# Splitting the last columns over two paths, and pieces of eight columns in place of four

## The chip, the cores and the metric

One core of one Trainium2 chip. The metric is the device time of one execution in microseconds (us), median over several executions, always compared with executions of the kernel before on the same chip in the same rounds. The profile is one execution taken by the hardware profiler; its span is about 1.7 us shorter than the measured time.

## The reference

The loss of a masked autoencoder: normalise every target patch, take the mean squared difference to the prediction, one number per image.

```python
batch, num_masked, dim = 32, 147, 768            # float32 inputs pred and target
mean = target.mean(axis=-1, keepdims=True)
var = target.var(axis=-1, keepdims=True)
target = (target - mean) / np.sqrt(var + 1e-6)
loss = np.mean((pred - target) ** 2, axis=-1)
return loss.mean(axis=-1).astype(np.float32)     # (32,)
```

## The kernel before

The 4704 patches lie as 36 full "columns" of 128 patches (one per partition) and a rest of 96. A column is 128 x 768 elements. All data is read once: the first target piece as float32 on a plain queue, nearly everything else on GpSimd's queue, which casts to bfloat16 on the way.

Work on a column c goes through four engines. VectorE takes the statistics of the target (two `bn_stats`, one `bn_aggr`), ScalarE the root, VectorE the reciprocal, GpSimd normalises:

```python
def normalise(u, c):                             # on GpSimd
    ...
    pin(nc.gpsimd.tensor_scalar(out=s[:n, so:so + D], in0=til[:n, o:o + D], scalar1=nm, scalar2=r,
                                op0=ALU.add, op1=ALU.mult))
```

Then the difference to the prediction and its square, on one of three paths, named in the list of units: "ACT" (TensorE forms p - s in PSUM with two identity matrices, ScalarE squares), "DVE+ACT" (VectorE subtracts, ScalarE squares), "DVE" (VectorE does both):

```python
def difference(u, d0, w):                        # two SBUF inputs
    ...
    pin(nc.vector.tensor_tensor(out=z[:, :w], in0=til[:, o:o + w], in1=s[:, so + d0:so + d0 + w],
                                op=ALU.subtract))

def square_dve(u, d0, w, dest):                  # reads z twice
    z = zs[u, d0][:, :w]
    pin(nc.vector.scalar_tensor_tensor(out=z, in0=z, scalar=1.0, in1=z, op0=ALU.mult, op1=ALU.mult,
                                       accum_out=dest))
```

The squares' row sums meet in a last small matmul per unit (`acc`), and 32 numbers are copied and written out. The order on each engine is fixed when the kernel is built: a list scheduler gives every operation an estimated duration, data arrival and rank, and emits them in the order of its estimated starts.

Of the kernel before, what the change touches and what calls it, by code (L numbers as in the profile page):

```python
# [7 lines left out]
F32 = mybir.dt.float32  # L8
BF16 = mybir.dt.bfloat16
ALU = mybir.AluOpType  # L10
ACTF = mybir.ActivationFunctionType
# [3 lines left out]
def kernel(  # L15
# [7 lines left out]
    nc = tc.nc  # L23
    pin = tc.keep_in_program_order
    B, N, D = pred.shape
    eps = 1e-6
    P = 128
    J = P // B
    KJ = (N + J - 1) // J
    KM = N - (J - 1) * KJ  # L30
    assert KJ == KM + 1
    RP = B * (J - 1)
    half = D // 2
    BANK = 512
    REST = KM
# [4 lines left out]
    def rows_of(c):  # L40
        return RP if c == REST else P

    data = ctx.enter_context(tc.tile_pool(name="data", bufs=1))
    work = ctx.enter_context(tc.tile_pool(name="work", bufs=16))
    diffs = ctx.enter_context(tc.tile_pool(name="diffs", bufs=4))
    small = ctx.enter_context(tc.tile_pool(name="small", bufs=8))
    singles = ctx.enter_context(tc.tile_pool(name="singles", bufs=1))
    psum = ctx.enter_context(tc.tile_pool(name="psum", bufs=2, space=bass.MemoryType.PSUM))
    psum1 = ctx.enter_context(tc.tile_pool(name="psum1", bufs=1, space=bass.MemoryType.PSUM))


# [3 lines left out]
    def piece(kind, c0, c1, d0=0, d1=D, q="sw"):  # L55
        stream.append((kind, c0, c1, d0, d1, q))

    piece("t", 0, 4, q="hw")
    piece("t", REST, REST + 1, q="hw2")
    piece("t", 4, 8)  # L60
    piece("p", REST, REST + 1)
    piece("t", 8, 12)
    piece("p", 0, 4)
    piece("t", 12, 16)
    piece("t", 16, 20)
    piece("p", 4, 8)
    piece("t", 20, 24)
    piece("t", 24, 28)
    piece("p", 8, 12)
    piece("t", 28, 32)  # L70
    piece("p", 12, 16)
    piece("t", 32, 36)
    for c in range(16, 32, 2):
        piece("p", c, c + 2)
    for c in range(32, 35):
# [6 lines left out]
    groups += [(c, c + 1) for c in range(16, KM, 2)]  # L82


    units = [((c, c + 1), 0, D, "ACT" if c < 18 else "DVE+ACT") for c in range(0, 24, 2)]
    units.insert(2, ((REST,), 0, D, "ACT"))
    units += [((24,), 0, D, "DVE"), ((25,), 0, D, "DVE+ACT"), ((26, 27), 0, D, "DVE+ACT")]
    units += [((c,), 0, D, "ACT" if c % 2 else "DVE") for c in range(28, KM - 1)]
    units += [((KM - 1,), 0, half, "ACT"), ((KM - 1,), half, D, "ACT")]



# [3 lines left out]
    def op(name, engine, dur, needs, fn, rank=0.0, early=0.0):  # L96
        by_name[name] = len(ops)
        ops.append((name, engine, dur, needs, fn, rank, early))
# [13 lines left out]
            KIND[kind].setdefault(c, []).append((d0, d1, til, (c - c0) * w))  # L112


    land, lanes, clock = {}, {"hw": [], "hw2": [], "sw": []}, 2.9
    for i, (kind, c0, c1, d0, d1, q) in enumerate(stream):
        w = (c1 - c0) * (d1 - d0)
        clock += w * rows_of(c0) / P * 0.915 / D + (0.0 if w >= 4 * D else 0.04)
        lanes[q].append(clock + 1.1)
        for c in range(c0, c1):  # L120
            land[kind, c, d0] = clock + 1.1
        k = len(lanes[q])
        op(("load", i), {"hw": "SP", "hw2": "ACT", "sw": "POOL"}[q], 0.6, [], lambda a=stream[i]: load(*a), rank=-1.0,
           early=0.0 if k <= 8 else lanes[q][k - 9] + 0.3)

    def landed(kind, c):
        return max(t for (k, cc, d), t in land.items() if k == kind and cc == c)

    ident = singles.tile([P, P], BF16)
# [25 lines left out]
    def bn(out, parts):  # L155

        n = parts[0].shape[0]
        st = small.tile([P, len(parts), 6], F32, name="st")
        for j, x in enumerate(parts):
            pin(nc.vector.bn_stats(out=st[:n, j, :], in_=x))  # L160
        pin(nc.vector.bn_aggr(out=out, in_=st[:n, :len(parts)]))  # L161

    def stats(g, i):
        n, K = rows_of(g[0]), len(g)
        if i == 0:
            mvs[g] = small.tile([P, K, 2], F32, name="mv")
        if not norm_pix_loss:
            return
        (_, _, til, o), = tbuf[g[i]]
        bn(mvs[g][:n, i], [til[:n, o + a:o + a + half] for a in (0, half)])  # L170
# [20 lines left out]

    for k, g in enumerate(groups):
        for i, c in enumerate(g):
            op(("bn", c), "DVE", 1.26, [], lambda g=g, i=i: stats(g, i), rank=k - 50.0, early=landed("t", c))
        op(("root", k), "ACT", 0.55, [("bn", c) for c in g], lambda g=g: root(g), rank=-1.0)
        op(("recip", k), "DVE", 0.2, [("root", k)], lambda g=g: recip(g), rank=-60.0)

# [16 lines left out]
    zs = {}  # L214
# [4 lines left out]

    def product(u, d0, w, src, so, eye, first):  # L220
        n, z = rows_of(u[0]), zs[u, d0]
        for a in range(0, w, BANK):
            b = min(w, a + BANK)
            pin(nc.tensor.matmul(z[:n, a:b], eye[:n, :n], src[:n, so + a:so + b], start=first, stop=not first))  # L224

    def sub_target(u, d0, w):
        if (u, d0) == units[-1][:2]:
            zs[u, d0] = psum1.tile([P, BANK], F32, name="z_last")
        else:
            zs[u, d0] = psum.tile([P, 3 * BANK], F32, name="z")  # L230
        s, so = sbuf[u[0]]
        product(u, d0, w, s, so + d0, nident, True)

# [7 lines left out]
    def difference(u, d0, w):  # L241

        z = zs[u, d0] = diffs.tile([P, 2 * D], BF16, name="zd")
        s, so = sbuf[u[0]]
        til, o = pred_of(u[0], d0)
        pin(nc.vector.tensor_tensor(out=z[:, :w], in0=til[:, o:o + w], in1=s[:, so + d0:so + d0 + w],  # L246
                                    op=ALU.subtract))

    def square_dve(u, d0, w, dest):
        z = zs[u, d0][:, :w]  # L250
        pin(nc.vector.scalar_tensor_tensor(out=z, in0=z, scalar=1.0, in1=z, op0=ALU.mult, op1=ALU.mult,  # L251
                                           accum_out=dest))

    tail = 5
    n_early = len(units) - 1 - tail
    rl = singles.tile([P, n_early], F32)
    rl_sum = singles.tile([P, 1], F32)
    finals = []
    early_ops, users, seen = [], [], set()
    for k, (u, d0, d1, eng) in enumerate(units):  # L260
        w = len(u) * D if len(u) > 1 else d1 - d0
        arrive = max(t for (kk, c, d), t in land.items() if kk == "p" and c in u and d < d1)
        norms = [("norm", c) for c in u]
        for c in u:
            if c not in seen:
                op(("norm", c), "POOL", 1.02, [("recip", group_of[c])], lambda u=u, c=c: normalise(u, c), rank=k)
                seen.add(c)
        if k < len(units) - tail:
            if u[0] == REST:
                dest = singles.tile([P, 1], F32, name="rl_rest")  # L270
                finals.append((("sq", k), dest, mask_rest, RP))
            else:
                dest = rl[:, len(early_ops):len(early_ops) + 1]
                early_ops.append(("sq", k))
        else:
            dest = singles.tile([P, 1], F32, name=f"rl{k}")
            finals.append((("sq", k), dest, mask, P))
        if eng in ("DVE", "DVE+ACT"):
            op(("diff", k), "DVE", 0.57 * w / D + 0.05, norms, lambda u=u, d0=d0, w=w: difference(u, d0, w), rank=-2.0,
               early=arrive)  # L280
            if eng == "DVE":
                op(("sq", k), "DVE", 1.0 * w / D, [("diff", k)],
                   lambda u=u, d0=d0, w=w, dest=dest: square_dve(u, d0, w, dest), rank=-1.0)
            else:
                op(("sq", k), "ACT", 0.75 * w / D + 0.25, [("diff", k)],
                   lambda u=u, d0=d0, w=w, dest=dest: square_act(u, d0, w, dest), rank=k)
            continue
        op(("subt", k), "PE", 0.37 * w / D, norms + (users[-2:-1] if k < len(units) - 1 else []) + ["ident"],
           lambda u=u, d0=d0, w=w: sub_target(u, d0, w), rank=k + 0.0)
        op(("pred", k), "PE", 0.37 * w / D, [("subt", k)], lambda u=u, d0=d0, w=w: add_pred(u, d0, w), rank=k,  # L290
           early=arrive)
        op(("sq", k), "ACT", 0.73 * w / D + 0.23, [("pred", k)],
           lambda u=u, d0=d0, w=w, dest=dest: square_act(u, d0, w, dest), rank=k)
        users.append(("sq", k))

    acc = psum1.tile([1, B], F32)
    def early_sum():
        junk = singles.tile([P, n_early], F32, name="junk")
        pin(nc.scalar.activation(out=junk, in_=rl, func=ACTF.Copy, accum_out=rl_sum))

    op("rl_sum", "ACT", 0.4, early_ops, early_sum, rank=50.0)
    finals.insert(0, ("rl_sum", rl_sum, mask, P))
    turn = []

    def final(vec, m, n):
        turn.append(n)
        pin(nc.tensor.matmul(acc, vec[:n], m[:n], start=len(turn) == 1, stop=len(turn) == len(finals)))  # L307

    for i, (need, vec, m, n) in enumerate(finals):
        op(("final", i), "PE", 0.2, [need, "masks"], lambda v=vec, m=m, n=n: final(v, m, n), rank=90.0)  # L310


    HOP = 0.15
# [3 lines left out]
    while left:  # L317
        best = None
        for i in left:
            name, engine, dur, needs, fn, rank, early = ops[i]  # L320
            if any(x not in end for x in needs):
                continue
            t = max([free[engine], early] + [end[x] + (0.0 if ops[by_name[x]][1] == engine else HOP) for x in needs])
# [4 lines left out]
        _, i, t = best  # L328
        name, engine, dur, needs, fn, rank, early = ops[i]
# [43 lines left out]
```

## Time and profile before

| | before |
|---|---|
| measured time, 6 runs of the comparison | 77.09 us (77.06 to 77.22) |
| span of the profiled execution | 75.4 us |
| DMA engines | full from 2 us to 71 us |
| VectorE / GpSimd busy | 75% / 72% of the span |
| TensorE / ScalarE busy | 40% / 42% |
| last data packet | 71.20 us |
| start of the final copy | 73.26 us |

The first lines to read are the slices of the DMA engines: a stream that never pauses sets the start of the end, and only what remains after its last packet can be shortened. The prediction below shows them, the end of the chain of waits, and VectorE beside GpSimd (start us, duration us, engine, line, operation). A line of the timeline gives start us, duration us, engine, line, operation.

```profile
63.04 0.55 DVE L246 TENSOR_TENSOR zd<-p,s 128x768 bf16<-128x768 bf16 x1
...
63.27 1.95 POOL L210 TENSOR_SCALAR s<-t,nm,r 128x768 bf16<-128x768 bf16 x1
63.51 0.95 DVE L251 SCALAR_TENSOR_TENSOR zd<-zd 128x768 bf16<-128x768 bf16 x1
```

The POOL line is one normalisation (x1), and it takes 1.95 us instead of 0.98. It began while a difference was running (to 63.59) and 0.24 us before VectorE's square, yet ended 0.97 us late. The difference overlaps it for only about 0.3 us; the rest of the delay lies beside the square, which itself shows nothing.

### The profile page before, as it was taken

What the parts mean: (1) busy time and instruction counts of PE and PEld (TensorE: products, weight loads), DVE (VectorE), ACT (ScalarE), POOL (GpSimd) and SP (SyncE); (2) the same over time, 40 slices, a digit from 0 to 9 for tenths busy, and PEclk for the clock granted to TensorE, in tenths of its full rate; (3) what the DMA queues carried; (4) which work ended last, traced back from release to release, by engine and by line L of the source; (5) the groups of instructions that cost most, each with busy time, mean ns of one, the idle gap of its engine ahead of it and who ended that gap; (6) DMA issues with size and microseconds to landing.
All of it is one profiled execution on the core that took longest, in us unless ns stands there. A gap on an engine that the chain in (4) does not pass through costs nothing.

```text
span 75.4 us, 570 instructions
## 1 busy us (share of the span) xinstructions
PE 30.3 (40%) x87; PEld 8.7 (11%) x88; DVE 56.3 (75%) x148; ACT 32.0 (42%) x73; POOL 54.4 (72%) x77
## 2 busy tenths in 40 slices
PE   0000000038596540688700778287544000348860
PEld 0000000001232110211100211031111000112220
DVE  0000099999999999976999928960999989989940
ACT  1400000210229802289210297239366099799550
POOL 4998205099999999499989898999878799800000
PEclk9999999999999997555555557965995555555555
DMA  0899999999999999999999999999999999999700
GB/s 0 215 424 339 262 192 236 218 209 215 212 215 215 212 216 225 212 209 215 215 212 215 219 212 225 209 212 202 214 215 209 215 210 210 214 205 205 117 0 0
DMA packets 3973, 15.41 MB, mean 204 GB/s; under 512 B 450, under 2 KB 1186, under 8 KB 3842
## 3 DMA queue, kind: packets, MB, share of 16 engines
q0 software_dynamic: 3712, 13.52, 89.2%
q1 hardware_dynamic: 146, 1.57, 5.7%
q10 hardware_dynamic: 112, 0.29, 1.0%
q14 instruction: 3, 0.02, 0.1%
HBM read 28.90 MB, written 0.00 MB: 383 GB/s over the span
## 4 chain that ended last, share of the span: by engine, by line
DMA 60%; DVE 18%; POOL 9%; issue 6%; PE 2%; ACT 1%; POOLq 0%; ACTq 0%
DMA t<-in_target_dram 49%; DVE st L160 14%; DMA p<-in_pred_dram 11%; POOL s L210 8%; DVE mv L161 3%; DVE zd L246 1%; PE acc L307 1%; POOL t L110 1%; PE z L224 1%; ACT z_last L239 1%; PE z_last L224 1%; POOLq L368 0%; DVE r L190 0%; POOL p L110 0%; DVE ob L336 0%
## 5 line engine op out<-in xcount | busy, mean ns | idle before, releaser
L160 DVE BATCH_NORM_STATS2 st<-t 128x6 f32<-128x384 bf16 (+2 forms) x74 | 36.3, 532 | 11.6 <-DMA t<-in_target_dram 11.6
L210 POOL TENSOR_SCALAR s<-t,nm,r 128x768 bf16<-128x768 bf16 (+2 forms) x37 | 38.2, 1040 | 3.2 <-ACT nm L185 2.0
L224 PE MATMUL z<-s,nident 128*128 128x512 bf16 (+4 forms) x36 | 14.6, 511 | 23.3 <-POOL s L210 17.6
L239 ACT ACTIVATE z<-z 128x1536 f32<-128x1536 f32 (+3 forms) x14 | 16.6, 1184 | 6.9 <-PE z L224 6.8
L224 PE MATMUL z<-p,ident 128*128 128x512 bf16 (+4 forms) x35 | 14.2, 542 | 12.1 <-DMA p<-in_pred_dram 12.0
L184 ACT ACTIVATE r<-mv,eps_t 128x2 f32<-128x2 f32 (+2 forms) x15 | 4.4, 293 | 29.5 <-DVE mv L161 28.8
L110 POOL DMA_DIRECT2D p<-in_pred_dram x18 | 10.2, 565 | 2.7 <-DVE st L160 1.0
L246 DVE TENSOR_TENSOR zd<-p,s 128x768 bf16<-128x768 bf16 (+1 forms) x10 | 9.7, 991 | 0.5 <-ACT zd L239 0.3
L161 DVE BATCH_NORM_AGGREGATE mv<-st 128x2 f32<-128x12 f32 (+1 forms) x37 | 7.7, 209 | 1.3
L110 POOL DMA_DIRECT2D t<-in_target_dram x8 | 4.9, 628 | 4.7 <-DMA t<-in_target_dram 3.9
L239 ACT ACTIVATE zd<-zd 128x1536 bf16<-128x1536 bf16 (+1 forms) x5 | 6.7, 1345 | 2.7 <-DVE zd L246 2.7
L224 PEld LDWEIGHTS <-ident 128*128 128x128 bf16 (+1 forms) x37 | 4.7, 126 | 27.2 <-issue 26.2
L224 PEld LDWEIGHTS <-nident 128*128 128x128 bf16 (+1 forms) x37 | 3.4, 114 | 34.6 <-issue 14.4
L251 DVE SCALAR_TENSOR_TENSOR zd<-zd 128x768 bf16<-128x768 bf16 x5 | 4.8, 955 | 0.1
L224 PE MATMUL z_last<-s,nident 128*128 128x384 bf16 x1 | 0.5, 479 | 7.1 <-POOL s L210 7.1
L190 DVE RECIPROCAL r<-r 128x2 f32<-128x2 f32 (+2 forms) x15 | 1.9, 123 | 1.7 <-ACT r L184 1.7
L185 ACT ACTIVATE nm<-mv 128x2 f32<-128x2 f32 (+2 forms) x15 | 2.8, 188 | 0.0
L239 ACT ACTIVATION_READ_ACCUMULATOR z<-z 128x1 f32 (+1 forms) x14 | 2.7, 190 | 0.0
L184 ACT ACT_TABLE_LOAD x1 | 1.3, 1283 | 1.5 <-PEq L354 1.5
L307 PE MATMUL acc<-mask,rl 128*1 128x32 f32 x10 | 1.0, 224 | 0.4 <-ACT z_last L239 0.4
L239 ACT ACTIVATION_READ_ACCUMULATOR zd<-zd 128x1 f32 x5 | 0.9, 187 | 0.0
L336 DVE COPY ob<-acc 1x32 f32<-1x32 f32 x1 | 0.2, 178 | 1.0 <-PE acc L307 1.0
(26 smaller groups left out, 5.8 us busy)
## 6 DMA issues: line engine op xcount, KB each, us to landing
t<-in_target_dram POOLq DMA_DIRECT2D x8, 768.0 KB, 24.5
p<-in_pred_dram POOLq DMA_DIRECT2D x4, 768.0 KB, 27.4
p<-in_pred_dram POOLq DMA_DIRECT2D x8, 384.0 KB, 20.9
t<-in_target_dram SPq DMA_DIRECT2D x1, 1536.0 KB, 8.4
p<-in_pred_dram POOLq DMA_DIRECT2D x3, 192.0 KB, 12.7
t<-in_target_dram ACTq DMA_DIRECT2D x1, 288.0 KB, 9.6
p<-in_pred_dram POOLq DMA_DIRECT2D x2, 96.0 KB, 7.3
p<-in_pred_dram POOLq DMA_DIRECT2D x1, 144.0 KB, 10.4
```

The lines of the kernel that those rows point to most:

```text
L110: pin(eng.dma_start(out=til[:n], in_=src))
L160: pin(nc.vector.bn_stats(out=st[:n, j, :], in_=x))
L161: pin(nc.vector.bn_aggr(out=out, in_=st[:n, :len(parts)]))
L184: pin(nc.scalar.activation(out=r[:n], in_=mv[:n, :, 1], func=ACTF.Sqrt, bias=eps_t[:n], scale=1.0))
L185: pin(nc.scalar.activation(out=nm[:n], in_=mv[:n, :, 0], func=ACTF.Copy, scale=-1.0))
L190: pin(nc.vector.reciprocal(out=rs[g][:n], in_=rs[g][:n]))
L210: pin(nc.gpsimd.tensor_scalar(out=s[:n, so:so + D], in0=til[:n, o:o + D], scalar1=nm, scalar2=r, op0=ALU.add, op1=ALU.mult))
L224: pin(nc.tensor.matmul(z[:n, a:b], eye[:n, :n], src[:n, so + a:so + b], start=first, stop=not first))
L239: pin(nc.scalar.activation(out=z[:n, :w], in_=z[:n, :w], func=ACTF.Square, accum_out=dest[:n]))
L246: pin(nc.vector.tensor_tensor(out=z[:, :w], in0=til[:, o:o + w], in1=s[:, so + d0:so + d0 + w], op=ALU.subtract))
L251: pin(nc.vector.scalar_tensor_tensor(out=z, in0=z, scalar=1.0, in1=z, op0=ALU.mult, op1=ALU.mult, accum_out=dest))
L307: pin(nc.tensor.matmul(acc, vec[:n], m[:n], start=len(turn) == 1, stop=len(turn) == len(finals)))
```

## The change

Its intent: fewer and larger transfers in the first half of the stream, and a shorter end, by cutting the last columns between ScalarE's path (the first 512 elements) and VectorE's (the other 256), in pairs with a strided access where there are two columns. It also lets the statistics of columns 32 to 35 wait behind differences, moves the early sum and the differences of columns 16 and 17 to VectorE, adds a fifth buffer for differences, divides PSUM anew for the split pieces, and re-estimates durations. Its core:

```diff
-    piece("t", 4, 8)
+    piece("t", 4, 12)
     piece("p", REST, REST + 1)
-    piece("t", 8, 12)
-    piece("p", 0, 4)
-    piece("t", 12, 16)
-    piece("t", 16, 20)
-    piece("p", 4, 8)
-    piece("t", 20, 24)
-    piece("t", 24, 28)
+    piece("t", 12, 20)
+    piece("p", 0, 8)
+    piece("t", 20, 28)
+    piece("t", 28, 32)
     piece("p", 8, 12)
 ...
-    units += [((24,), 0, D, "DVE"), ((25,), 0, D, "DVE+ACT"), ((26, 27), 0, D, "DVE+ACT")]
-    units += [((c,), 0, D, "ACT" if c % 2 else "DVE") for c in range(28, KM - 1)]
-    units += [((KM - 1,), 0, half, "ACT"), ((KM - 1,), half, D, "ACT")]
+    units += [((24,), 0, D, "DVE"), ((25,), 0, D, "DVE+ACT")]
+    for u in [(c, c + 1) for c in range(26, KM - 4, 2)] + [(c,) for c in range(KM - 4, KM - 1)]:
+        units += [(u, 0, BANK, "ACT"), (u, BANK, D, "DVE")]
+    units += [((KM - 1,), 0, half, "ACT"), ((KM - 1,), half, D, "DVE")]
 ...
-            op(("bn", c), "DVE", 1.26, [], ..., rank=k - 50.0, early=landed("t", c))
+            op(("bn", c), "DVE", 1.26, [], ..., rank=k - 50.0 if c < 32 else -1.5, early=landed("t", c))
 ...
+            y = til[:, o - d0:o - d0 + K * D].rearrange("p (k d) -> p k d", d=D)[:, :, d0:d0 + e]
+            v = s[:, so:so + K * D].rearrange("p (k d) -> p k d", d=D)[:, :, d0:d0 + e]
 ...
-    op("rl_sum", "ACT", 0.4, early_ops, early_sum, rank=50.0)
+    op("rl_sum", "DVE", 0.2, early_ops, ...tensor_reduce..., rank=-3.0)
```

More of the change, by code (lines that the diff above doesn't have):

```diff
@@ L44 @@
     work = ctx.enter_context(tc.tile_pool(name="work", bufs=16))
-    diffs = ctx.enter_context(tc.tile_pool(name="diffs", bufs=4))
+    diffs = ctx.enter_context(tc.tile_pool(name="diffs", bufs=5))
     small = ctx.enter_context(tc.tile_pool(name="small", bufs=8))
     singles = ctx.enter_context(tc.tile_pool(name="singles", bufs=1))
-    psum = ctx.enter_context(tc.tile_pool(name="psum", bufs=2, space=bass.MemoryType.PSUM))
     psum1 = ctx.enter_context(tc.tile_pool(name="psum1", bufs=1, space=bass.MemoryType.PSUM))
@@ L59 @@
     piece("t", REST, REST + 1, q="hw2")
-    piece("t", 4, 8)
+    piece("t", 4, 12)
     piece("p", REST, REST + 1)
-    piece("t", 8, 12)
-    piece("p", 0, 4)
-    piece("t", 12, 16)
-    piece("t", 16, 20)
-    piece("p", 4, 8)
-    piece("t", 20, 24)
-    piece("t", 24, 28)
+    piece("t", 12, 20)
+    piece("p", 0, 8)
+    piece("t", 20, 28)
+    piece("t", 28, 32)
     piece("p", 8, 12)
-    piece("t", 28, 32)
+    piece("t", 32, 36)
     piece("p", 12, 16)
-    piece("t", 32, 36)
     for c in range(16, 32, 2):
@@ L82 @@
     groups += [(c, c + 1) for c in range(16, KM, 2)]
-    units = [((c, c + 1), 0, D, "ACT" if c < 18 else "DVE+ACT") for c in range(0, 24, 2)]
+    units = [((c, c + 1), 0, D, "ACT" if c < 16 else "DVE+ACT") for c in range(0, 24, 2)]
     units.insert(2, ((REST,), 0, D, "ACT"))
-    units += [((24,), 0, D, "DVE"), ((25,), 0, D, "DVE+ACT"), ((26, 27), 0, D, "DVE+ACT")]
-    units += [((c,), 0, D, "ACT" if c % 2 else "DVE") for c in range(28, KM - 1)]
-    units += [((KM - 1,), 0, half, "ACT"), ((KM - 1,), half, D, "ACT")]
+    units += [((24,), 0, D, "DVE"), ((25,), 0, D, "DVE+ACT")]
+    for u in [(c, c + 1) for c in range(26, KM - 4, 2)] + [(c,) for c in range(KM - 4, KM - 1)]:
+        units += [(u, 0, BANK, "ACT"), (u, BANK, D, "DVE")]
+    units += [((KM - 1,), 0, half, "ACT"), ((KM - 1,), half, D, "DVE")]
     ops, by_name = [], {}
@@ L112, in load @@
             KIND[kind].setdefault(c, []).append((d0, d1, til, (c - c0) * w))
-    land, lanes, clock = {}, {"hw": [], "hw2": [], "sw": []}, 2.9
+    land, lanes, clock = {}, {"hw": [], "hw2": [], "sw": []}, 2.8
     for i, (kind, c0, c1, d0, d1, q) in enumerate(stream):
@@ L193 @@
         for i, c in enumerate(g):
-            op(("bn", c), "DVE", 1.26, [], lambda g=g, i=i: stats(g, i), rank=k - 50.0, early=landed("t", c))
+            op(("bn", c), "DVE", 1.26, [], lambda g=g, i=i: stats(g, i), rank=k - 50.0 if c < 32 else -1.5, early=landed("t", c))
         op(("root", k), "ACT", 0.55, [("bn", c) for c in g], lambda g=g: root(g), rank=-1.0)
@@ L221, in product @@
         n, z = rows_of(u[0]), zs[u, d0]
-        for a in range(0, w, BANK):
-            b = min(w, a + BANK)
-            pin(nc.tensor.matmul(z[:n, a:b], eye[:n, :n], src[:n, so + a:so + b], start=first, stop=not first))
+        runs = [(0, so, w)] if w % D == 0 else [(k * BANK, so + k * D, w // len(u)) for k in range(len(u))]
+        for zo, o, e in runs:
+            for a in range(0, e, BANK):
+                b = min(e, a + BANK)
+                pin(nc.tensor.matmul(z[:n, zo + a:zo + b], eye[:n, :n], src[:n, o + a:o + b],
+                                     start=first, stop=not first))
     def sub_target(u, d0, w):
-        if (u, d0) == units[-1][:2]:
-            zs[u, d0] = psum1.tile([P, BANK], F32, name="z_last")
-        else:
-            zs[u, d0] = psum.tile([P, 3 * BANK], F32, name="z")
+        if u in pairs_pe:
+            zs[u, d0] = pools["pairs"].tile([P, 3 * BANK], F32, name="z")
+            pairs_pe.remove(u)
+        else:
+            if "parts" not in pools:
+                pools["stack"].close()
+                pools["parts"] = ctx.enter_context(tc.tile_pool(name="parts", bufs=3, space=bass.MemoryType.PSUM))
+            zs[u, d0] = pools["parts"].tile([P, 2 * BANK], F32, name="zp")
         s, so = sbuf[u[0]]
@@ L245, in difference @@
         til, o = pred_of(u[0], d0)
-        pin(nc.vector.tensor_tensor(out=z[:, :w], in0=til[:, o:o + w], in1=s[:, so + d0:so + d0 + w],
-                                    op=ALU.subtract))
+        K, e = len(u), w // len(u)
+        if e == D:
+            x, y, v = z[:, :w], til[:, o:o + w], s[:, so:so + w]
+        elif K == 1:
+            x, y, v = z[:, :w], til[:, o:o + w], s[:, so + d0:so + d0 + w]
+        else:
+            x = z[:, :w].rearrange("p (k d) -> p k d", d=e)
+            y = til[:, o - d0:o - d0 + K * D].rearrange("p (k d) -> p k d", d=D)[:, :, d0:d0 + e]
+            v = s[:, so:so + K * D].rearrange("p (k d) -> p k d", d=D)[:, :, d0:d0 + e]
+        pin(nc.vector.tensor_tensor(out=x, in0=y, in1=v, op=ALU.subtract))
     def square_dve(u, d0, w, dest):
@@ L252, in square_dve @@
                                            accum_out=dest))
-    tail = 5
+    tail = 4
     n_early = len(units) - 1 - tail
@@ L257 @@
     rl_sum = singles.tile([P, 1], F32)
+    pairs_pe = [u for u, d0, d1, eng in units if eng == "ACT" and (u[0] == REST or len(u) * (d1 - d0) > 2 * BANK)]
+    n_pairs = len(pairs_pe)
+    pools = {"stack": ExitStack()}
+    pools["pairs"] = pools["stack"].enter_context(tc.tile_pool(name="psum", bufs=2, space=bass.MemoryType.PSUM))
     finals = []
-    early_ops, users, seen = [], [], set()
+    early_ops, users, dusers, seen = [], [], [], set()
     for k, (u, d0, d1, eng) in enumerate(units):
-        w = len(u) * D if len(u) > 1 else d1 - d0
+        w = len(u) * (d1 - d0)
         arrive = max(t for (kk, c, d), t in land.items() if kk == "p" and c in u and d < d1)
@@ L278 @@
         if eng in ("DVE", "DVE+ACT"):
-            op(("diff", k), "DVE", 0.57 * w / D + 0.05, norms, lambda u=u, d0=d0, w=w: difference(u, d0, w), rank=-2.0,
+            op(("diff", k), "DVE", 0.57 * w / D + 0.05, norms + dusers[-5:-4], lambda u=u, d0=d0, w=w: difference(u, d0, w), rank=-2.0,
                early=arrive)
+            dusers.append(("sq", k))
             if eng == "DVE":
@@ L284 @@
             else:
-                op(("sq", k), "ACT", 0.75 * w / D + 0.25, [("diff", k)],
+                op(("sq", k), "ACT", 0.65 * w / D + 0.22, [("diff", k)],
                    lambda u=u, d0=d0, w=w, dest=dest: square_act(u, d0, w, dest), rank=k)
             continue
-        op(("subt", k), "PE", 0.37 * w / D, norms + (users[-2:-1] if k < len(units) - 1 else []) + ["ident"],
+        op(("subt", k), "PE", 0.37 * w / D, norms + (users[-2:-1] if len(users) < n_pairs else users[n_pairs - 1:n_pairs] + users[n_pairs:][-3:-2]) + ["ident"],
            lambda u=u, d0=d0, w=w: sub_target(u, d0, w), rank=k + 0.0)
@@ L291 @@
            early=arrive)
-        op(("sq", k), "ACT", 0.73 * w / D + 0.23, [("pred", k)],
+        op(("sq", k), "ACT", 0.65 * w / D + 0.22, [("pred", k)],
            lambda u=u, d0=d0, w=w, dest=dest: square_act(u, d0, w, dest), rank=k)
@@ L296 @@
     acc = psum1.tile([1, B], F32)
-    def early_sum():
-        junk = singles.tile([P, n_early], F32, name="junk")
-        pin(nc.scalar.activation(out=junk, in_=rl, func=ACTF.Copy, accum_out=rl_sum))
-    op("rl_sum", "ACT", 0.4, early_ops, early_sum, rank=50.0)
+    op("rl_sum", "DVE", 0.2, early_ops, lambda: pin(nc.vector.tensor_reduce(
+        out=rl_sum, in_=rl, axis=mybir.AxisListType.X, op=ALU.add)), rank=-3.0)
     finals.insert(0, ("rl_sum", rl_sum, mask, P))
@@ L309 @@
     for i, (need, vec, m, n) in enumerate(finals):
-        op(("final", i), "PE", 0.2, [need, "masks"], lambda v=vec, m=m, n=n: final(v, m, n), rank=90.0)
+        op(("final", i), "PE", 0.2, [need, "masks"], lambda v=vec, m=m, n=n: final(v, m, n), rank=90.0,
+           early=max(land.values()) + 0.4)
     HOP = 0.15
```

## The prediction

> **What bounds the kernel now.** I first read the page's slices and its DMA lines: does the stream ever pause?
>
> ```profile
> DMA  0899999999999999999999999999999999999700
> GB/s 0 215 424 339 262 192 236 218 209 215 212 215 215 212 216 225 212 209 215 215 212 215 219 212 225 209 212 202 214 215 209 215 210 210 214 205 205 117 0 0
> ...
> q0 software_dynamic: 3712, 13.52, 89.2%
> ```
>
> From about 2 us to 71 us the DMA engines are full. The GB/s count what is written: on the casting queue a float32 column is read and half its bytes written, so 212 written is 424 read. By the packet records of the trace, pieces of four columns end 3.662 us apart, pieces of two 1.855 us and single columns 0.951 us. From 4d + f = 3.662 and 2d + f = 1.855: d = 0.9035 us a column and f = 0.048 us a transfer (d + f = 0.951 fits the third). The last packet ends at 71.2 us. Nothing that only moves work while the stream runs shortens the span, unless it shows after the last packet. So I next read the end of the chain of waits (start us, us, what).
>
> ```profile
> 62.66 8.34 DMA p<-in_pred_dram
> 71.00 0.04 issue
> 71.05 0.48 PE z L224
> 71.53 0.33 PE acc L307 x4
> 71.85 0.45 PE z_last L224
> 72.30 0.02 issue
> 72.32 0.47 ACT z_last L239
> ...
> 72.96 0.28 PE acc L307 x2
> 73.23 0.02 issue
> 73.26 0.18 DVE ob L336
> ```
>
> The tail is 2.26 us from 71.00 to the copy at 73.26, then about 2.1 us of result transfer to the span's end at 75.4, which the change leaves alone. The tail is the two half columns through TensorE and ScalarE, with a first batch of final sums (0.33) in between. The third view is the timeline of VectorE and GpSimd over the last 18 us.
>
> ```profile
> 57.38 1.94 POOL L210 TENSOR_SCALAR s<-t,nm,r 128x768 bf16<-128x768 bf16 x2
> 57.45 2.69 DVE L246 TENSOR_TENSOR zd<-p,s 128x1536 bf16<-128x1536 bf16 x1
> ...
> 60.13 1.80 DVE L246 TENSOR_TENSOR zd<-p,s 128x1536 bf16<-128x1536 bf16 x2
> ...
> 60.42 2.29 POOL L210 TENSOR_SCALAR s<-t,nm,r 128x768 bf16<-128x768 bf16 x1 [0.59 <-DVE r L190]
> ...
> 69.24 0.55 DVE L246 TENSOR_TENSOR zd<-p,s 128x768 bf16<-128x768 bf16 x1
> ...
> 69.83 0.96 DVE L251 SCALAR_TENSOR_TENSOR zd<-zd 128x768 bf16<-128x768 bf16 x1
> ...
> 70.71 0.55 DVE L246 TENSOR_TENSOR zd<-p,s 128x768 bf16<-128x768 bf16 x1
> ```
>
> Two things are to be seen. A difference that arrives while GpSimd normalises is held until GpSimd has finished both back-to-back normalisations: it starts at 57.45 and ends at 60.14, which is 0.82 us after GpSimd ended at 59.32. The other way round, the normalisation at 60.42 takes 2.29 instead of about 0.98 behind two differences. And VectorE is barely ahead of the data: a column's difference and square take 1.47 us (69.24 to 70.71), more than the 0.951 us between landings; it ends only a little before ScalarE.
>
> **What the Trainium skill says.** "DMA: Bandwidth & Descriptors", section "Where 436 GB/s comes from", gives 435 GB/s as the ceiling of the ports into SBUF. One column, 393,216 bytes read, in 0.9035 us is 435 GB/s, so the rate has nothing left; only the 0.048 us a transfer can be saved. The same page, "Queues, rings and completion order", says that an engine takes turns between queues a packet at a time. The trace agrees: between 6 and 8 us packets of the first target piece (plain queue, 0.473 us) alternate with packets of the casting queue (also 0.473). "SBUF — State Buffer", "Who interferes with whom": a VectorE instruction with two SBUF inputs contends with a GpSimd instruction that reads SBUF, because its second input uses the shared read interface. The timeline above agrees for the difference. The square at 63.51, which reads one tile twice, ran 0.95 beside a normalisation, so I let it pass unhindered. "VectorE: DVE Perf Modes", "The perf-mode tier table", gives tensor_tensor in bf16 twice the plain rate; the trace has 0.55 for 768 elements, which is that. No run yet shows a strided one.
>
> **The change part by part.**
>
> Stream. Four pairs of four-column pieces become four pieces of eight: 22 casting transfers instead of 26. By f that is 4 x 0.048 = 0.19 us earlier for everything from the second half on; the last packet ends at about 71.0. GpSimd issues four fewer (0.56 each), which is hidden. Expected cost: a casting packet now takes about 0.95 us per turn, so the first target piece, with two packets per engine left when that queue starts, lands 0.9 us later than 9.2, and the first eight casting columns land together at about 15.3. VectorE, at 1.13 us per column, needs those at 15 to 16: hidden. Its statistics of columns 4 to 19 then end at 34.1, while columns 20 to 27 land at 37.7: an idle of nearly 4 us. All targets land at 48.7 instead of 52.5, so the statistics of column 32 still end near 53.1, before prediction pair 16 is seen at 54.5. The idle is paid back before the tail.
>
> Tail work. Moving units to other paths changes VectorE's work. Differences: before 4 pairs and 6 singles, 10,752 elements per row; after 4 pairs, 2 singles, three of 512, three of 256, one of 384, 10,368. Squares: 3,840 before, 3,456 after. That is only 0.6 us less work (384/1.92 + 384/0.96), and 3 more instructions of either kind, each with about 0.1 us fixed, which is as much again. VectorE gains nothing; but it now also has the last half column, and the statistics of 33 to 35 lie between differences instead of ahead of them.
>
> The order that decides. In the built order VectorE runs: statistics 35, difference (28,29), square 24, reciprocal of (34,35), difference (30,31). Difference (28,29) waits for its prediction, seen at 65.5 (before: 65.7). Add 0.4 for it, 0.88 for the square of 768 and 0.11 for the reciprocal: 66.9. This releases GpSimd's last two normalisations, with no issue left between them: 67.0 to 68.95. Prediction pair 30 is seen at 67.4, in the middle of them. By the pattern at 57.45 the difference is held to 68.95. From there, with squares at n/960 + 0.08 us (0.88 for 768, as measured) and independent differences at n/1920 + 0.10 (0.90 for 1536, the two at 60.13): difference (30,31) 69.25; square of 512 69.86; difference 32 70.09; square 70.70; difference 33 70.93; square 71.54; difference 34 71.77; two squares of 256 72.47; the early sum, now on VectorE, 72.67; difference of the last half 72.97; square of 256 73.32; square of 384 73.80, its accumulator 73.88. Then 0.32 for the last final sum and 0.04: the copy starts at 74.24, against 73.26. The sum is +0.98 us: 77.13 + 0.98 = 78.1 us. ScalarE, with 512 instead of 768 elements for each last column and the first half column only, ends near 72.2 and sets nothing.
>
> **The rivals.**
>
> First rival: no hold. GpSimd's pieces let VectorE in, or the reciprocal comes early enough. Then difference (30,31) runs at 67.4, later differences follow their landings (68.5, 69.4, 70.3), and the same additions from 70.3 give the copy at about 73.0: a gain of 0.2 to 0.3 us, 76.9 us. For it: the two queues share the work as intended, and no final sum stands before the last product any more. Against: the three differences that arrived during a normalisation (57.45, 62.17, 64.38) were all held. Half a hold (VectorE gets in after the first normalisation) is +0.0 to +0.2: 77.2.
>
> Second rival: the stream itself. If larger packets ran better than d and f say, the end could come another 0.3 us earlier; if the late start of the first piece or the 4 us idle were not paid back, the end would come 1 us later. For the former speaks nothing at 435 GB/s; against the latter speaks VectorE's wait of 1.3 us for pair 16, by which it is level again.
>
> Third rival: the strided differences lose the double rate. Then each of the three costs 0.27 us more; only the last of them lies behind the hold, so 78.4 us; more if VectorE's gaps turn out smaller than I have them.
>
> **Range and chances.** I give the hold about 65 in 100 (78.1, with the third rival 78.4), no hold or half a hold 35 (76.8 to 77.3). I place the time a little under the first: 77.9 us. The range is 76.7 to 78.6. Faster by over 2% means under 75.6, a gain of 1.55; even a last half handled without any backlog (0.35 to be seen, 0.30, 0.48, 0.08, 0.32, 0.04 after 71.0) puts the copy at 72.6, a gain of 0.7. So 3 in 100. Slower by over 2% means over 78.67, which needs the hold, slow strided differences and a little more: 14 in 100. Within 2%: 83.
>
> **What would show each step.** Four fewer transfers: 3136 packets on the casting queue and the last packet at 71.0. First piece: VectorE's first statistics near 10 instead of 9.25, a wait of about 4 us near 34 to 38. The hold: a difference of 512 elements that starts near 67.4 and lasts some 1.8 us, beside two normalisations from 67.0. The end: VectorE busy without gaps to 73.9, the chain through its squares rather than ScalarE's z_last, the copy at 74.2. I am wrong if that difference lasts 0.4 us, if the chain still ends on ScalarE or on the last landing, or if the last packet has moved by more than 0.4 us.

## The result

78.01 us median (77.83 to 78.20, 6 runs) against 77.09: the ratio is 1.0116, with a 95% interval of 1.0099 to 1.0132. It is slower by about 1.2%, inside 2%. Ratios here are the mean time of one kernel's fast runs over that of the other's fast runs of the same rounds, so they are not quite the ratio of the medians.

The profiled execution of the changed kernel (78.2 us, span 76.5 us) first, its DMA lines:

```profile
DMA  0899899999999999999999999999999999999000
...
DMA packets 3397, 15.41 MB, mean 201 GB/s; under 512 B 386, under 2 KB 1122, under 8 KB 2754
...
q0 software_dynamic: 3136, 13.52, 86.9%
```

The stream is as full as before, with 3136 packets on the casting queue instead of 3712. Its last packet came at 71.34 us, 0.14 later than before in this execution. The end of its chain of waits (start us, us, what):

```profile
53.22 14.54 DMA p<-in_pred_dram
67.76 0.03 issue
...
71.97 0.70 DVE zd L264 x4
...
72.76 0.06 DVE rl_sum L315
72.83 0.04 issue
72.87 0.36 DVE zd L260
73.23 0.83 DVE zd L264 x4
74.06 0.04 issue
74.10 0.23 PE acc L322 x2
74.34 0.02 issue
74.36 0.18 DVE ob L353
```

Before, the chain left the DMA at 71.00 and ended on ScalarE. Now it leaves the DMA at 67.76 already, for prediction pair 30, and is VectorE's from there to 74.06: 6.3 us in which no landing was waited for long enough to matter. VectorE is the engine that ends the kernel, and the copy starts at 74.36 instead of 73.26. Why it is behind shows in the timeline from 67.8 us, VectorE and GpSimd together:

```profile
67.84 3.38 POOL L206 TENSOR_SCALAR s<-t,nm,r 128x768 bf16<-128x768 bf16 x2 [3.38 <-DVE r L186]
67.86 0.43 DVE L260 TENSOR_TENSOR zd<-p,s 128x512 bf16<-128x512 bf16 x1 [0.23 <-DMA p<-in_pred_dram]
68.21 0.68 DVE L264 SCALAR_TENSOR_TENSOR zd<-zd 128x512 bf16<-128x512 bf16 x1
...
68.82 0.90 DVE L260 TENSOR_TENSOR zd<-p,s 128x256 bf16<-128x256 bf16 x1
...
70.25 0.28 DVE L260 TENSOR_TENSOR zd<-p,s 128x256 bf16<-128x256 bf16 x1
...
70.46 1.30 DVE L264 SCALAR_TENSOR_TENSOR zd<-zd 128x512 bf16<-128x512 bf16 x1
```

GpSimd's last two normalisations take 3.38 us together instead of 1.95. On VectorE a difference of 256 takes 0.90 (the same shape at 70.25: 0.28) and a square of 512 takes 1.30 (the same shape at 68.21: 0.68). Each lost 0.62 us, 1.24 together, at a place where the stream is nearly over. That is a little more than the 1.10 by which the copy is later.

### The profile page after: what moved, and what is told of

Read it like the earlier page. It is cut to its first block, busy times and chain, and to the rows that moved or that the text cites. A ratio compares the mean times of both kernels' runs of the same rounds, so it can differ in the third digit from the quotient of the medians.

```text
span 76.5 us, 575 instructions
## 1 busy us (share of the span) xinstructions
PE 28.4 (37%) x84; PEld 8.8 (12%) x84; DVE 57.3 (75%) x158; ACT 32.1 (42%) x73; POOL 53.5 (70%) x73
## 3 DMA queue, kind: packets, MB, share of 16 engines
q0 software_dynamic: 3136, 13.52, 86.9%
## 4 chain that ended last, share of the span: by engine, by line
DMA 64%; DVE 25%; issue 4%; POOL 3%; PE 0%; DVEq 0%; POOLq 0%
DMA t<-in_target_dram 45%; DMA p<-in_pred_dram 19%; DVE st L156 16%; DVE mv L157 3%; DVE zd L264 3%; DVE zd L260 3%; POOL t L106 2%; POOL p L106 1%; PE acc L322 0%; DVE r L186 0%; DVE ob L353 0%; DVE rl_sum L315 0%; DVEq L315 0%; DVEq L260 0%; POOLq L371 0%
## 5 line engine op out<-in xcount | busy, mean ns | idle before, releaser
L223 PE MATMUL z<-s,nident 128*128 128x512 bf16 (+2 forms) x26 | 10.3, 502 | 23.4 <-POOL s L206 20.2
L244 ACT ACTIVATE z<-z 128x1536 f32<-128x1536 f32 (+1 forms) x9 | 12.3, 1365 | 5.6 <-PE z L223 5.6
L223 PE MATMUL z<-p,ident 128*128 128x512 bf16 (+2 forms) x26 | 9.2, 495 | 12.6 <-DMA p<-in_pred_dram 12.6
L260 DVE TENSOR_TENSOR zd<-p,s 128x1536 bf16<-128x1536 bf16 (+4 forms) x13 | 10.4, 818 | 1.9 <-POOL s L206 1.4
L223 PE MATMUL zp<-p,ident 128*128 128x512 bf16 (+1 forms) x10 | 5.3, 588 | 4.2 <-DMA p<-in_pred_dram 4.2
L223 PE MATMUL zp<-s,nident 128*128 128x512 bf16 (+1 forms) x10 | 5.3, 589 | 4.0 <-ACT z L244 2.4
L244 ACT ACTIVATE zp<-zp 128x1024 f32<-128x1024 f32 (+2 forms) x7 | 5.2, 750 | 0.2 <-PE zp L223 0.2
L264 DVE SCALAR_TENSOR_TENSOR zd<-zd 128x512 bf16<-128x512 bf16 (+3 forms) x8 | 5.3, 676 | 0.0
L106 POOL DMA_DIRECT2D t<-in_target_dram x5 | 3.2, 671 | 0.8 <-POOLq L371 0.8
L244 ACT ACTIVATION_READ_ACCUMULATOR zp<-zp 128x1 f32 x7 | 1.3, 189 | 0.0
```

Of the source, the lines that this page charges most:

```text
L106: pin(eng.dma_start(out=til[:n], in_=src))
L223: pin(nc.tensor.matmul(z[:n, zo + a:zo + b], eye[:n, :n], src[:n, o + a:o + b], start=first, stop=not first))
L244: pin(nc.scalar.activation(out=z[:n, :w], in_=z[:n, :w], func=ACTF.Square, accum_out=dest[:n]))
L260: pin(nc.vector.tensor_tensor(out=x, in0=y, in1=v, op=ALU.subtract))
```

## The experiments

**Question.** My theory: the loss is the hold, the last two normalisations and VectorE's differences and squares keeping each other out of SBUF. Rivals: VectorE simply has too much work at the end; the split makes it so; the pieces of eight or the last landing do it. Each number below is a ratio to the kernel before; "x us gained" is the changed kernel's ratio minus the run's, times 77.1 us. The runs came in three sets, each on a chip of its own, so such a difference carries both intervals: about 0.2 us for most runs, 0.5 for e3. In e1 and h1 every instruction left on VectorE, TensorE and ScalarE keeps its place; in the other runs the list scheduler also moves instructions.

| run | what it is | median us | ratio (95%) |
|---|---|---|---|
| changed kernel | | 78.01 | 1.0116 (1.0099 to 1.0132) |
| e1_skip_late_norm | neither late normalisation | 76.93 | 0.9964 (0.9947 to 0.9980) |
| h1_skip_one_norm | only one of them | 77.23 | 1.0019 (1.0003 to 1.0035) |
| e5_late_norm_dve | both on VectorE | 77.73 | 1.0073 (1.0058 to 1.0088) |
| e2_pieces4 | pieces of four, split kept | 77.27 | 1.0010 (0.9984 to 1.0035) |
| e3_pieces8 | before, with pieces of eight | 78.60 | 1.0174 (1.0117 to 1.0231) |
| e4_stats_first | late rank undone | 77.07 | 0.9992 (0.9965 to 1.0019) |
| f1_split20 | one piece of eight cut | 77.07 | 0.9987 (0.9966 to 1.0008) |
| g2_best_try | f1 and PSUM buffers | 76.67 | 0.9960 (0.9921 to 0.9998) |
| g2_again | the same kernel | 76.99 | 0.9991 (0.9974 to 1.0008) |
| g5_lastquarter | g2 with a smaller last part | 77.14 | 1.0016 (0.9986 to 1.0045) |

**Take the normalisations away.** Columns 34 and 35 read what was normalised for 32 and 33. This computes something wrong; the loss is a mean over so much random data that the result still stays within the tolerance of the comparison.

```diff
+    alias = {34: 32, 35: 33}
-        s, so = sbuf[u[0]]
+        s, so = sbuf[alias.get(u[0], u[0])]
-            if c not in seen:
+            if c not in seen and c not in alias:
```

> The changed kernel without the last two normalisations on GpSimd: columns 34 and 35 read the normalised columns 32 and 33 instead, so the result is wrong on purpose; every other instruction and its order stay. Theory (the hold: the last two normalisations and VectorE's differences and squares shut each other out of SBUF): the difference that took 0.90 us and the square that took 1.30 us fall back to 0.28 and 0.68, the copy comes at about 73.1 instead of 74.36, and the time is 76.6 to 77.0 us. Rival (VectorE has simply too much work at the end): under 0.3 us is gained, 77.7 us or more. Rival (the later last landing, 71.34 against 71.20): 0.14 us at most is at stake, and this run leaves it as it is.

Measured: 76.93 us, 1.17 us gained ((1.0116 - 0.9964) x 77.1). VectorE's order is unchanged, and in its timeline the two stretched instructions are back at their usual length:

```profile
68.65 0.29 DVE L261 TENSOR_TENSOR zd<-p,s 128x256 bf16<-128x256 bf16 x1
...
69.88 0.68 DVE L265 SCALAR_TENSOR_TENSOR zd<-zd 128x512 bf16<-128x512 bf16 x1
...
73.21 0.18 DVE L354 COPY ob<-acc 1x32 f32<-1x32 f32 x1 [0.31 <-PE acc L323]
```

In the changed kernel the differences of columns 34 and 35 need these two normalisations, but they began at 71.69 and 72.87, when the normalisations had ended (69.58 and 71.22). So two GpSimd instructions for which VectorE never stood idle cost the kernel 1.2 us, more than the 0.9 us (0.0116 x 77.1) that the change lost. "Too much work at the end" falls: the work is the same here. The last packet came at 71.18 us in e1's execution, so a later landing is worth 0.16 us of this at most.

**Take only one away.**

```diff
-    alias = {34: 32, 35: 33}
+    alias = {35: 33}
```

> The changed kernel without only the last of the two late normalisations: column 35 reads the normalised column 33, so the result is wrong on purpose; instruction order otherwise as changed. Theory (hold): with one of the two late normalisations left, one stretched VectorE instruction (about 0.6 us) stays and one goes: 77.3 to 77.6 us, half way between 78.01 and 76.93. Rival (the loss comes from the normalised column arriving late at TensorE, not from the shared access): skipping the later one gives all of the gain or none.

Measured: 77.23 us, slightly better than expected. Of the two stretched instructions the difference keeps its 0.90 us and the square is at 0.68 again: one normalisation, one stretch. The two shares are 0.75 us for the later one and 0.42 for the earlier. Their difference is hardly larger than the error of such a figure. A part of it shows in the trace of e1: with both gone, the differences at 69.67 and 70.55 start 0.20 and 0.06 us later than right behind their predecessors, which those of h1 (69.95 and 70.77) do not, so not all of the second 0.62 could be gained.

**Move them instead.** GpSimd's instruction becomes VectorE's; the result is right.

```diff
-                op(("norm", c), "POOL", 1.02, [("recip", group_of[c])], ..., rank=k)
+                if 34 <= c < KM:
+                    op(("norm", c), "DVE", 0.35, [("recip", group_of[c])], ... nc.vector ..., rank=-59.0)
+                else:
+                    op(("norm", c), "POOL", 1.02, [("recip", group_of[c])], ..., rank=k)
```

> The changed kernel with the normalisations of columns 34 and 35 on VectorE right after their reciprocal, instead of on GpSimd. Correct result. Theory (hold): VectorE takes 2 x 0.3 to 0.35 us more but loses no 1.25 us: net gain 0.55 to 0.65, 77.3 to 77.5 us, with no difference or square stretched after 66 us. Rival (VectorE's work at the end is the bound as such): 0.6 us slower, 78.6.

Measured: 77.73 us, 0.33 gained; the expected gain was nearly twice that. No difference or square is stretched after 66 us, as the theory has it, and the rival's 78.6 is far off. The size was wrong at the other end: the two normalisations took 0.87 us on VectorE (0.48 and 0.475, a little overlapped), not 0.6 to 0.7, and what they save is 1.17, not 1.25.

**Undo the pieces alone**, with the piece list of before and everything else changed.

```diff
-    piece("t", 4, 12)          # ... and so on: the list of after
+    piece("t", 4, 8)           # ... the list of before
```

> The split last columns with the pieces of before (four columns): undoes the stream part alone. Theory: all that costs is the late release of the last two normalisations, and it comes from how the schedule falls with pieces of eight; with pieces of four they are released near 63.5 us, ahead of the tail, so the time is 76.6 to 76.9 us, faster than before, and the last packet is back at 71.2. Rival (the split itself is what costs, through more and shorter instructions on VectorE): 77.7 us or more.

Measured: 77.27 us, no different from before and 0.8 us better than the changed kernel. The 77.7 of the rival is refuted: with these pieces the split and all else in the change cost nothing that this run resolves. But my 76.6 to 76.9 is missed too. The late normalisations came from 63.8 to 67.2, where VectorE has slack, and then the next thing ended the kernel: ScalarE, whose chain reads

```profile
67.84 1.02 PE zp L227 x2
...
68.89 0.87 ACT zp L248
...
70.06 1.05 PE zp L227 x2
...
71.19 0.70 ACT zp L248 x2
...
73.17 0.29 PE acc L326 x4
```

TensorE ran here at a granted clock of 0.5 (a pair's two products take 1.02 us), and at 70.06 it had waited 0.35 us for ScalarE to free a PSUM buffer. Which of the two kept the expected gain away was not tested.

**Do the pieces alone**, on the kernel before.

```diff
-    piece("t", 4, 8)           # ... the list of before
+    piece("t", 4, 12)          # ... the list of after
```

> The kernel before with pieces of eight columns: the stream part alone. Theory: the same trap in weaker form, since the first statistics of columns 20 to 27 start 4 us late and the last normalisations fall into the tail: 77.4 to 78.0 us. Rival (the stream part is harmless, or saves its four transfers): 76.9 to 77.1. The last packet near 71.3 in either case.

Measured: 78.60 us (77.88 to 79.02), slower than the kernel before and than I expected. Its interval reaches 1.0117, into that of the changed kernel (to 1.0132), so it is not shown to be worse than the whole change. The same hold, with another victim:

```profile
66.15 2.60 POOL L206 TENSOR_SCALAR s<-t,nm,r 128x768 bf16<-128x768 bf16 x1
66.17 0.95 DVE L247 SCALAR_TENSOR_TENSOR zd<-zd 128x768 bf16<-128x768 bf16 x1
...
67.06 0.95 DVE L247 SCALAR_TENSOR_TENSOR zd<-zd 128x768 bf16<-128x768 bf16 x1
...
68.81 0.48 PE L220 MATMUL z_last<-s,nident 128*128 128x384 bf16 x1 [8.39 <-POOL s L206]
```

Now GpSimd waits: the last normalisation takes 2.60 us behind two squares. TensorE's fixed order had the subtraction of that column ahead of the products of earlier ones, so TensorE stood idle for 8.39 us, ScalarE's squares came late, and the copy at 74.78. The pieces alone are harmful to the order that the old tail gets; whether the split tail takes some of that back is not shown.

**Cut only the piece that made VectorE wait.** In the changed kernel VectorE waits at the third piece of eight:

```profile
38.29 1.02 DVE L156 BATCH_NORM_STATS2 st<-t 128x6 f32<-128x384 bf16 x2 [1.94 <-DMA t<-in_target_dram]
```

```diff
-    piece("t", 20, 28)
+    piece("t", 20, 24)
+    piece("t", 24, 28)
```

> The changed kernel with the third piece of eight target columns (20 to 27) cut into two pieces of four again, everything else as changed. Theory: the piece of eight at this place makes VectorE wait from 35.6 to 38.3 us, that wait is what pushes the statistics of columns 33 to 35 in between the differences and so the last two normalisations to 67 us; with the piece cut, the wait shrinks to under 1 us, the reciprocal of (34,35) comes near 63.5 and both normalisations are over by 66.5: no held difference or square after 68 us, and 76.9 to 77.3 us. Rival (it is the split of the last columns and the order of their statistics, whatever the pieces): within 0.2 us of the changed kernel, 77.8 us or more.

Measured: 77.07 us, 0.99 gained, the number as expected. Its reciprocal of (34,35) came at 63.43 instead of 67.47, the stretched instructions (two squares of 512 at 65.07 and 66.76, 1.30 and 1.28 us) lie before 68 us, and the chain ends on ScalarE at 72.8. A hold of the same size, four us earlier, cost nothing that shows.

The wait, however, did not shrink to under 1 us. VectorE stood idle for 1.84 us (0.44 and 1.40), now for ScalarE's roots, against 2.35 us (0.41 and 1.94) in the changed kernel:

```profile
34.47 0.17 DVE L187 RECIPROCAL r<-r 128x2 f32<-128x2 f32 x1 [0.44 <-ACT r L181]
...
40.64 0.17 DVE L187 RECIPROCAL r<-r 128x2 f32<-128x2 f32 x1 [1.40 <-ACT r L181]
```

What changed is the built order: the statistics of column 33 now stand ahead of the first difference, that of pair 16, and only those of 34 and 35 (57.70, 61.36) lie between differences, where the changed kernel has three (57.99, 61.66, 65.10). The scheduler makes that order from estimated landings, before anything runs. So the run shows that the piece matters, and points to the order rather than to VectorE's wait on the chip. The next run separates the two: it changes ranks alone and leaves that wait as it is.

**Undo the late rank alone**, keeping all pieces of eight.

```diff
-            op(("bn", c), ..., rank=k - 50.0 if c < 32 else -1.5, early=landed("t", c))
+            op(("bn", c), ..., rank=k - 50.0, early=landed("t", c))
```

> The changed kernel with the statistics of columns 32 to 35 at the same high rank as all others, as before the change: undoes the late rank alone, pieces of eight stay. Theory: the statistics end near 57.5, but the differences then run in one row from 58 to 64 and shut out GpSimd's normalisations instead, which fall to 64 to 68.5: only little is gained, 77.5 to 77.9 us. Rival (the late rank is the cause by itself): 76.8 to 77.1 us.

Measured: 77.07 us, 0.96 gained, though VectorE still stood idle for 2.60 us at the piece of eight (0.61, 0.41 and 1.58, up to 38.03). So the wait on the chip is not what costs; the place of the statistics in the built order is. All of them now stand ahead of the first difference. My expectation is wrong and the rival's number is right. I had the differences shut GpSimd out for so long that its normalisations fell into the tail; in the trace six differences did run in one row (58.65 to 65.0), but GpSimd got through in between (one normalisation of 2.94 us, then two in 2.38 us). Only the last one reached 66.43 to 67.98, where VectorE was waiting for prediction pair 30 anyway, and the difference at 67.68 lost 0.13 us. So neither the piece of eight nor the late rank alone costs anything that these runs resolve in this tail; each removes the loss when undone. It takes both to put two normalisations after 67 us.

**A version better than both?** With the hold gone the next bound was ScalarE's chain with TensorE's waits for PSUM. So f1 with one-bank buffers for the single columns, and column 33 left out of the early sum (left out of the cut: the pairs keep two buffers of two banks, and TensorE's waits are adapted):

```diff
+                pools["ones"] = ctx.enter_context(tc.tile_pool(name="ones", bufs=3, space=bass.MemoryType.PSUM))
+            if len(u) > 1:
+                zs[u, d0] = pools["parts"].tile([P, 2 * BANK], F32, name="zp")
+            else:
+                zs[u, d0] = pools["ones"].tile([P, BANK], F32, name="z1")
-    tail = 4
+    tail = 6
```

> A try at a version that beats both: the cut piece of the first run of this set, and the last single columns in one-bank PSUM buffers of their own (three of them, with two two-bank buffers for the pairs), so that TensorE's subtraction for a column need not wait for ScalarE's square of three units before; the early sum leaves out column 33. Theory: after the hold is gone ScalarE's last squares end the kernel, and these waits of TensorE (0.3 to 0.6 us in the run with pieces of four) go: 76.6 to 76.9 us. Rival (the last landing and ScalarE's own work bind): as the cut piece alone.

Measured: 76.67 us, and a profiled execution whose chain is short: last landing seen at 71.44, difference, square, final sum, copy at 72.85. But the executions spread from 76.46 (mean granted clock of TensorE 0.931) to 77.52 (0.791), and the interval almost touches 1. So again, together with a smaller last part:

> The try at a better version once more, since its first interval reached from 0.992 to 0.9998 and its executions spread from 76.46 to 77.52. Expected: 76.5 to 76.9 us, faster than before by 0.3 to 0.7%.

Measured: 76.99 us, ratio 0.9991. The gain is not confirmed; the expected 0.3 to 0.7% was missed. Its chain ended on ScalarE, with the granted clock at 0.50 to 0.52 from 62 to 70 us and the copy at 73.03.

```diff
-    units += [((KM - 1,), 0, half, "ACT"), ((KM - 1,), half, D, "DVE")]
+    units += [((KM - 1,), 0, BANK, "ACT"), ((KM - 1,), BANK, D, "DVE")]
```

> The same with the last column cut at 512 instead of 384: 256 elements are left for VectorE after the last landing. Its chain now ends landing, difference, square, final sum, and the two VectorE instructions take 0.36 and 0.56 us. With 256 elements 0.29 and 0.42: 0.2 us less, 76.4 to 76.7 us, unless the 512 of ScalarE (0.58 instead of 0.48, after a later landing) end last: then no gain.

Measured: 77.14 us, no gain: the chain ends on ScalarE's larger part at 72.76, the case that the expectation named. I have no version that is shown to beat the kernel before among those with a right result; the best, f1, e4 and g2, are level with it or faster by less than these runs resolve.

## Why the prediction was right, and which of its steps were not

The time, the direction and the engine were right: 78.1 us for the hold, 77.9 as the stated value, 78.01 measured; the copy at 74.24 predicted, 74.36 in the trace; the chain on VectorE. The experiments carry the kind of cause: without the two normalisations the loss is gone (76.93), without one most of it (77.23). That the copy came within 0.12 us is in part luck: prediction pair 30 was seen at 67.86 instead of 67.4, 0.46 later, and the hold cost 1.24 us instead of 1.55, 0.31 less. And the prediction's own sign of being wrong, that the difference at 67.4 lasts 0.4 us, came true: it lasted 0.43. The hold fell on other instructions.

- **The stream.** 3136 packets as predicted. Pieces of eight end 7.277 us apart in the packet records of the changed kernel, where 8d + f is 7.276: the second rival's faster large packets are not there. One reading does not hold as put: 435 GB/s is what the stream reads, while the ceiling named beside it is that of the ports into SBUF, and only half of it, 218 GB/s, is written there. That "the rate has nothing left" does not follow from that ceiling. The last packet at 71.0 was not what this execution showed (71.34). Over the profiles, with pieces of eight throughout (six kernels, 70.99 to 71.34, mean 71.13) and with pieces of four throughout (two, 71.20 and 71.36, mean 71.28), the difference is 0.15 us, near the 0.19 of the prediction, but single executions scatter more than that.
- **The first piece.** Predicted 0.9 us later than 9.2; VectorE's first statistics started at 10.98 instead of 9.25, so 1.73 later. The term was mis-sized: casting packets of 12,288 bytes took 0.926 us, near the 0.95 assumed, and the piece's last data packet ended at 9.59 us instead of 8.29; but its completion packet takes a turn as well, which I had not counted, and came at 10.63 instead of 8.88. It stayed hidden, as predicted.
- **The wait at 34 to 38 us "is paid back before the tail".** It was 2.35 us, not nearly 4: the statistics of columns 4 to 19 ended at 35.77 instead of 34.1. On VectorE it was paid back: the statistics of column 32 ended at 53.44 (53.1 predicted), and the difference of pair 16 began at 54.88 after 1.41 us of idleness. But this is the step that does not stand as put. The prediction knew that the statistics of 33 to 35 lie between differences; it did not see that the piece of eight has a part in that, through the built order. f1 cuts the piece and moves the statistics of 33 ahead, e4 moves all three ahead and keeps the wait (2.60 us): the loss is gone in both. The wait itself was harmless; the estimated landing behind it, through the order, put another engine's work in a worse place.
- **The release of the last normalisations.** Predicted 66.9, in the trace 67.63. The differences of 24, 25 and the pair (26,27) were themselves held behind normalisations (the three took 2.36 us from 62.82), which I did not carry on into the end.
- **The hold.** Predicted: one difference, (30,31), held from 67.4 to 68.95, 1.55 us. In the trace that difference started 0.01 us after the normalisation and took its usual 0.43; a later difference and a square were held for 0.62 each. "I let it pass unhindered", of the square, was wrong: the square contends both ways, as the POOL line at 63.27 of the kernel before suggests. Which instructions are held was wrong, the sum (1.24 against 1.55) was near.
- **The strided differences** keep the double rate: two runs of 256 took 0.43 us where 256 in one run took 0.28, that is 0.15 us for 256 more, near 256/1920 = 0.13. The third rival falls.

The first rival, no hold, describes e1: 76.9 us and the copy at 73.0 predicted for it, 76.93 and 73.21 measured. So the additions without the hold were good to about 0.2 us, and the collision accounts for the whole loss.

## What to carry to other kernels

When VectorE and GpSimd both read SBUF, treat an instruction of VectorE with two SBUF inputs and one of GpSimd as sharing a resource, and look where they meet: in f1 a hold that ended before 68 us was free, in the changed kernel one of the same size after that cost 1.17 us of its 1.24. If a scheduler fixes the order, a larger transfer early in the stream can decide where they meet at its end; look at the releases of the last operations on each engine, not only at whether the waiting engine catches up. And before blaming a change's headline part, undo each part by itself: here two parts, each harmless in this tail, made the loss together.

## What the Trainium skill lacked or had wrong

- "SBUF — State Buffer", section "Who interferes with whom", says that a VectorE instruction with two SBUF inputs contends with a GpSimd instruction that reads SBUF. The runs agree, and add that it holds for `scalar_tensor_tensor` with the same tile as both inputs (1.30 us instead of 0.68), and that the loss is mutual (normalisations of 1.74 and 1.65 us instead of 0.98).
- The same section says that issue order decides who blocks, for whole instructions. It does not say who gets in next when both sides have more queued. In these runs two normalisations in a row kept a difference out for both (2.69 us at 57.45 in the kernel before), two squares in a row kept a normalisation out (2.60 us in e3), but a difference that began 0.01 us after a normalisation was not held at all (0.43 us at 67.86 in the changed kernel).
- "DMA: Bandwidth & Descriptors", section "Queues, rings and completion order", says that queues take turns by the packet. What the section leaves out is that the row length of one queue's transfers sets the other's share: with rows of 12,288 bytes written (0.926 us a packet) in place of 6144 (0.474), the first piece on the plain queue was used 1.73 us later; and that the completion packet waits its turn too.
- The same page gives a fixed part of about 2 us per DMA (section "Anatomy of one DMA — SWDGE (gpsimd) path") and asks for 1 MiB or more (section "Bandwidth"). In a queue that is kept full the cost of one more transfer here was 0.048 us, and transfers of 384 KB written (two columns in 1.855 us) read at 424 GB/s.
